# The low parts of the weight tiles, made once, stored to DRAM and loaded again by later token groups

## The chip, the cores and the metric

One Trainium2 chip, one of its cores. The time is the device time of one execution in microseconds; the smaller the better. All numbers are fp32, and the weights and activations that go through the projections are split into two parts so that TensorE's products keep fp32's precision.

## What is computed

One step of a diffusion backbone of one layer, for 128 prompt tokens and 2048 latent tokens of 1024 channels:

```python
def trunk_layer(x, cond, S0, ada_w, ada_b, norm_g, w_in, ...):
    mod = jax.nn.silu(cond) @ ada_w + ada_b
    shift, scale, gate = jnp.split(mod, 3, axis=-1)
    h = rmsnorm(x, norm_g) * (1 + scale[:, None]) + shift[:, None]
    p = h @ w_in                                   # one projection, columns for four branches
    qkv, g_a, beta_logit, a_logit, uv, g_b, x_c, g_c, x_d, g_d = jnp.split(p, _split_points(), axis=-1)
    y_a, S_new = deltanet_branch(...)              # gated delta rule: triangular solves, then a scan over chunks of 64
    y_b = sgu_branch(...)                          # spatial gating over 128 positions
    y_c = pool_branch(...)                         # centred averages of 2, 4, 8, 16
    y_d = fourier_branch(...)                      # real 2-D DFT over positions and channels
    out = jnp.concatenate([y_a, y_b, y_c, y_d], axis=-1) @ w_out
    return x + gate[:, None] * out, S_new
```

The change lies in `h @ w_in` alone: in how the weights of that product reach TensorE.

## The kernel before

**Tokens.** The 34 chunks of 64 tokens form three groups (0, 1, 2 with 12, 12 and 10 chunks). The split activations of one group, `hT`, lie in SBUF at a time; the weights are streamed past them. So every weight tile is brought in three times, once for each group.

**Weight tiles.** `load_w(src, n)` (L220 to L244) fills one slot of a ring of three slots in the SBUF tile BIG. A tile has 128 columns of all eight k blocks of 128 rows: 512 KB. It is loaded in two halves of four k blocks (`wst`, 256 KB each, a pool of two buffers, issued on SP's queue at L238). From each half two parts are made: `hi`, the value rounded to the fp32r type (a cast, on ACT at L242 in the first stages, on DVE at L240 once `Ring.late` is set), and `lo`, the rest `w - hi` (a subtract at L243: on DVE for the first half, on GpSimd, called POOL in the profile, for the second). `mm3` (L246 to L250) then makes three matmuls for each k block, hi by hi, hi by lo and lo by hi: 24 for one output chunk of 256 or more tokens. `proj_cm` (L486) works on two tiles at once and takes their chunks in turn, `proj_tm` (L475) on one. Two kinds of tiles are wider: `wxd` with 272 columns, and `wv` with 256 columns (1 MB, in two slots).

**Order of the work.** Phase A, up to about 450 us, goes through groups 0, 1 and 2 with wxd, the two pooling tiles `wxc_d` (which an earlier step has written to DRAM) and wt0 to wt5 (queries, keys, values), and makes the triangular solves of the delta rule (L725, L727). A later phase, called R here, goes through groups 2, 1 and 0 with the gate tiles wt6 to wt15 and `wv`. Between its projections stand the 32 steps of the scan over the latent chunks (L1015 to L1066, its matmuls at L1035, its loads of R and C at L1024 and L1026). The output projection (L1349 on, it uses L250 too) is last.

**What sets the order.** The kernel is written as a sequence of tiles, and a scheduler puts the instructions of each engine in order by a simulated time line and by priorities; `load_w` runs at a raised priority (`hp(OXv[1])`, 500), the matmuls at priority 0. Every load and store is issued on SP's one queue, in order: an issue that waits for a semaphore keeps back all that stand behind it. The completions use eight semaphores in turn, so each transfer also waits for the one eight before it.

Of the kernel before, what the change touches and what calls it, by code (L numbers as in the profile page):

```python
# [9 lines left out]
F32 = mybir.dt.float32  # L10
# [4 lines left out]
ALU = mybir.AluOpType  # L15
# [7 lines left out]
KC = D // 128  # L23
# [121 lines left out]
def tile_dit_step(ctx: ExitStack, tc: tile.TileContext, io: dict, dbg=None, stop=None):  # L145
    nc = tc.nc
# [5 lines left out]
    dram = ctx.enter_context(tc.tile_pool(name="dram", bufs=1, space=DR))  # L152
# [60 lines left out]
    def hp(o):  # L213
        return tc.high_priority(offset=o)
# [5 lines left out]
    def load_w(src, n):  # L220
        with hp(OXv[1]):
            ns = -(-n // SLOT)
            if ns == 1:
                s = Ring.order.pop(0)
                Ring.order.append(s)
            else:
                s = min(0, 1) if Ring.order.index(2) != 0 else 1
                for q in (s, s + 1):
                    Ring.order.remove(q)
                    Ring.order.append(q)  # L230
            hi = Wr[0][:, :, s * SLOT:s * SLOT + n]
            lo = Wr[1][:, :, s * SLOT:s * SLOT + n]
            for a in range(0, n, 136):
                w = min(136, n - a)
                for k0 in range(0, KC, 4):
                    ks = slice(k0, k0 + 4)
                    st = wst_p.tile([128, 4, SLOT], F32, tag="wst", name="wst")
                    nc.sync.dma_start(out=st[:, :, :w], in_=src[:, ks, a:a + w])  # L238
                    if Ring.late:
                        nc.vector.tensor_copy(hi[:, ks, a:a + w], st[:, :, :w])  # L240
                    else:
                        nc.scalar.activation(hi[:, ks, a:a + w], st[:, :, :w], AF.Copy)  # L242
                    (nc.vector if k0 == 0 else nc.gpsimd).tensor_tensor(lo[:, ks, a:a + w], st[:, :, :w], hi[:, ks, a:a + w].bitcast(F32), op=ALU.subtract)  # L243
            return hi, lo  # L244

    def mm3(out, lh, rh, ks=range(KC), first=0, last=KC - 1):  # L246
        with hp(OP):
# [122 lines left out]
    with tc.tile_pool(name="ada", bufs=3, reuse_waits="tile") as ada_p:  # L370
# [59 lines left out]
        p1 = x_prep([(i, 128) for i in range(3)], 0, 0, ada_p)  # L430
        a1 = ada_load(1)
        w_xd = load_w(io["wxd"], 272)
        with hp(300):
            mod_q(0, a0)
# [40 lines left out]
    def proj_tm(src, n, tiles, dst, w=None, done=()):  # L475
        hi, lo = w or load_w(src, n)
        for j, i in enumerate(tiles):
            if j < len(done):
                dst(j, i, done[j])
                continue  # L480
            ps = pj()
            mm3(ps[:, :n], [lambda k, q=q: hT[q][:, k, j * 128:(j + 1) * 128] for q in range(2)],
                [lambda k: hi[:, k], lambda k: lo[:, k]])
            dst(j, i, ps)

    def proj_cm(srcs, chunks, dsts):  # L486
        ws = [load_w(src, 128) for src in srcs]
        for (a, w) in chunks:
            for (hi, lo), dst in zip(ws, dsts):
                ps = pj()  # L490
                mm3(ps[:, :w], [lambda k: hi[:, k], lambda k: lo[:, k]],
                    [lambda k, q=q: hT[q][:, k, a:a + w] for q in range(2)])
                dst(a, w, ps)
                tick()
# [825 lines left out]
    op = [ctx.enter_context(tc.tile_pool(name="opa_", bufs=1, side="right", reuse_waits="tile"))]  # L1320
# [15 lines left out]
    for k in range(KC):  # L1336
        st = op[0].tile([128, D], F32, tag="wos", name="wos", bufs=2)
        nc.sync.dma_start(out=st, in_=io["wo"][k * 128:k * 128 + 128])
        st = st.rearrange("p (n j) -> p n j", j=256)
# [91 lines left out]
```

## Time and profile before

| | |
|---|---|
| three timed runs | 1191.8, 1192.86 (median), 1195.96 us |
| the profiled execution | 1198.78 us, of which the profiled span is 1197.0 us |
| mean granted TensorE clock | 0.919 of full speed |
| TensorE busy | 1046.3 us of the span (87%) |
| VectorE (DVE) busy | 818.9 us (68%) |
| GpSimd (POOL) busy | 433.2 us (36%) |
| bytes moved by SP's queue | 202.37 MB |

Busy times are sums over stages that differ: TensorE has almost no pause in some stretches of 50 us and stands for a quarter of others. The chain of waits, which is followed back from the last instruction, tells what the end of the span rested on; the windows tell, stage by stage, which engine is full.

### The profile page before, as it was taken

How to read it: one execution, taken by the hardware profiler on the slowest of the kernel's cores; microseconds unless marked ns; L12 is line 12 of the kernel's file. 1: busy time of each engine (PE TensorE's matmuls, PEld its weight loads, DVE VectorE, ACT ScalarE, POOL GpSimd, SP SyncE). 2: the span in 40 equal slices, each digit the busy share in tenths (PEclk: the TensorE clock that was granted, in tenths of full speed). 3: DMA queues.
4: the chain of work that ended last, by engine and by line, in shares of the span. 5: the costliest groups of instructions: out<-in, count | busy, mean ns of one | idle time of the engine just before them, and what ended most of it. 6: DMA issues, size and time to landing. Idle time of an engine off the chain costs nothing.

```text
span 1197.0 us, 27975 instructions
## 1 busy us (share of the span) xinstructions
PE 1046.3 (87%) x11351; PEld 954.6 (80%) x11351; DVE 818.9 (68%) x1837; ACT 386.2 (32%) x734; POOL 433.2 (36%) x436
## 2 busy tenths in 40 slices
PE   4689897888768789967988999888999889999997
PEld 1489786888757788955778888878899879999997
DVE  1547878699995799958865533672443398887765
ACT  1345566436675564131131111121111311111211
POOL 1338446633562245511132132232144444332212
PEclk7599897898978899988899999999999889999998
DMA  9799557854453655565268356578555655444331
GB/s 309 238 327 290 156 117 202 250 165 112 107 134 103 154 126 126 179 170 160 71 197 241 100 170 207 176 230 283 143 151 161 204 153 186 132 142 140 108 131 71
DMA packets 251395, 204.16 MB, mean 171 GB/s; under 512 B 109150, under 2 KB 218718, under 8 KB 251010
## 3 DMA queue, kind: packets, MB, share of 16 engines
q1 hardware_dynamic: 251266, 202.37, 57.7%
q8 instruction: 89, 1.46, 0.5%
q14 instruction: 40, 0.33, 0.1%
HBM read 138.86 MB, written 63.46 MB: 169 GB/s over the span
## 4 chain that ended last, share of the span: by engine, by line
PE 41%; DVE 27%; DMA 17%; issue 6%; ACT 4%; SPq 2%; POOL 2%; DVEq 0%; ACTq 0%; POOLq 0%
PE pj L250 32%; DMA wst<-in_wt_dram 4%; PE pa L1035 3%; DMA ada<-in_ada_dram 3%; DVE LL L727 3%; DVE acc L824 3%; DVE ltmp L725 3%; DMA pr<-in_cpr_dram 2%; DVE BIG L243 2%; DVE BIG L361 1%; DVE acc L871 1%; SPq L1024 1%; DVE BIG L240 1%; DVE BIG L362 1%; DVE LL L748 1%
## 5 line engine op out<-in xcount | busy, mean ns | idle before, releaser
L250 PE MATMUL pj<-BIG 128*128 128x256 f32 (+4 forms) x3888 | 630.8, 319 | 25.6 <-ACT raw L805 5.6
L250 PEld LDWEIGHTS pj<-BIG 128*128 128x128 f32 x3888 | 578.1, 201 | 50.7 <-issue 11.0
L250 PE MATMUL pj<-BIG,yh 128*128 128x256 f32 x1088 | 196.7, 286 | 1.6 <-ACT BIG L1340 0.8
L243 POOL TENSOR_TENSOR BIG<-wst,BIG 128x512 fp32r<-128x512 f32 (+1 forms) x66 | 93.3, 1414 | 215.2 <-DVE BIG L240 131.2
L250 PEld LDWEIGHTS pj<-BIG,yh 128*128 128x128 f32 x1088 | 164.7, 191 | 4.6 <-ACT BIG L1340 1.0
L250 PE MATMUL pj<-BIG,yl 128*128 128x256 f32 x544 | 140.8, 284 | 0.0
L250 PEld LDWEIGHTS pj<-BIG,yl 128*128 128x128 f32 x544 | 99.0, 191 | 0.4
L240 DVE CAST BIG<-wst 128x512 fp32r<-128x512 f32 (+2 forms) x72 | 35.0, 487 | 75.7 <-DMA wst<-in_wt_dram 35.4
L1398 POOL TENSOR_TENSOR z<-z,xs 128x1024 f32<-128x1024 f32 x16 | 40.3, 2521 | 75.8 <-DVE z L1390 66.0
L1042 POOL TENSOR_TENSOR gS<-S,sc_s 128x256 f32<-128x256 f32 x32 | 19.7, 616 | 132.1 <-DVE S L1057 109.1
L824 DVE SCALAR_TENSOR_TENSOR acc<-raw,prm,acc 128x768 f32<-128x768 f32 (+2 forms) x72 | 66.3, 942 | 1.6 <-ACT acc L822 1.6
L243 DVE TENSOR_TENSOR BIG<-wst,BIG 128x512 fp32r<-128x512 f32 (+1 forms) x66 | 49.8, 754 | 24.3 <-ACT BIG L242 20.7
L1359 ACT ACTIVATE yh<-yt 128x768 fp32r<-128x768 f32 (+1 forms) x34 | 20.5, 628 | 121.6 <-issue 65.5
L1204 ACT ACTIVATE g<-pj 128x256 f32<-128x256 f32 (+1 forms) x64 | 23.0, 397 | 109.6 <-PE pj L250 109.3
L725 DVE TENSOR_TENSOR ltmp<-LL 128x60 f32<-128x60 f32 (+14 forms) x90 | 55.5, 617 | 1.6
L727 DVE TENSOR_TENSOR LL<-LL,ltmp 128x60 f32<-128x60 f32 (+14 forms) x90 | 55.3, 615 | 1.5
L242 ACT ACTIVATE BIG<-wst 128x512 fp32r<-128x512 f32 (+1 forms) x60 | 37.7, 633 | 38.4 <-DMA wst<-in_wt_dram 17.9
L264 PE MATMUL pb<-ada,c 128*32 128x256 f32 x192 | 22.1, 566 | 31.7 <-DMA ada<-in_ada_dram 21.4
L1057 DVE TENSOR_TENSOR S<-pa,gS 128x256 f32<-128x256 f32 x34 | 14.3, 421 | 50.6 <-PE pc L1035 45.3
L1390 DVE TENSOR_TENSOR z<-pj,gbc 128x256 f32<-128x256 f32 x68 | 26.2, 420 | 29.1 <-PE pj L250 28.8
L362 POOL TENSOR_TENSOR BIG<-h,BIG 128x384 fp32r<-128x384 f32 (+2 forms) x28 | 29.1, 1041 | 44.5 <-DVE BIG L361 38.7
L1360 DVE TENSOR_TENSOR yl<-yt,yh 128x768 fp32r<-128x768 f32 (+1 forms) x34 | 40.4, 1206 | 4.1 <-ACT yh L1359 3.9
(280 smaller groups left out, 1690.2 us busy)
## 6 DMA issues: line engine op xcount, KB each, us to landing
wst<-in_wt_dram SPq DMA_DIRECT2D x96, 256.0 KB, 3.7
R<-rec_d SPq DMA_DIRECT2D x136, 128.0 KB, 3.0
ada<-in_ada_dram SPq DMA_DIRECT2D x24, 512.0 KB, 8.7
C<-com_d SPq DMA_DIRECT2D x68, 128.0 KB, 3.2
xs<-xs_d SPq DMA_DIRECT2D x16, 512.0 KB, 5.3
out_dram<-z SPq DMA_DIRECT2D x16, 512.0 KB, 3.0
x<-in_xs_dram SPq DMA_DIRECT2D x13, 512.0 KB, 6.4
xs_d<-x SPq DMA_DIRECT2D x13, 512.0 KB, 4.7
```

Of the source, the lines that this page charges most:

```text
L240: nc.vector.tensor_copy(hi[:, ks, a:a + w], st[:, :, :w])
L242: nc.scalar.activation(hi[:, ks, a:a + w], st[:, :, :w], AF.Copy)
L243: (nc.vector if k0 == 0 else nc.gpsimd).tensor_tensor(lo[:, ks, a:a + w], st[:, :, :w], hi[:, ks, a:a + w].bitcast(F32), op=ALU.subtract)
L250: nc.tensor.matmul(out, lh[a](k), rh[b](k), start=(k == first and i == 0), stop=(k == last and i == 2))
L362: (nc.gpsimd if f % 2 else nc.vector).tensor_tensor(hT[1][:, f, off:off + w], h, hi.bitcast(F32), op=ALU.subtract)
L725: nc.vector.tensor_tensor(tv, X[:, :, j, j + 1:32].unsqueeze(2).to_broadcast([128, 2, j, ni]), bc(X[:, :, 0:j, j], ni), op=ALU.mult)
L727: nc.vector.tensor_tensor(X[:, :, 0:j, j + 1:32], X[:, :, 0:j, j + 1:32], tv, op=ALU.add)
L824: nc.vector.scalar_tensor_tensor(o, raw[:, si + j:si + j + n], w[:, j:j + 1], o, op0=ALU.mult, op1=ALU.add)
L1035: nc.tensor.matmul(ps[o, q], lh(q)[hp], rh[hp, q])
L1360: nc.vector.tensor_tensor(yl[:, q], yt[:, q], yh[:, q].bitcast(F32), op=ALU.subtract)
L1390: nc.vector.tensor_tensor(z[:, ns], ps, gbc[:, cd, ns], op=ALU.mult)
L1398: nc.gpsimd.tensor_tensor(z, z, xs, op=ALU.add)
```

## The change

The first group that makes a tile still subtracts; when its `lo` is complete, one DMA writes it to a DRAM tile of its own (`lo_d`, 512 KB, or 1 MB for `wv`). For later groups the tile counts as `kept`: its `lo` is not computed but loaded from there, straight into the slot in BIG. The DMA for it is written ahead of the loads of `wst`, and it has to wait for the last matmul that reads the slot's old content. The halves of w are still loaded in every group, and `hi` is still cast from them. The 272 column tile is left as it was.

```diff
--- before.py
+++ after.py
@@ -230,6 +230,10 @@
                     Ring.order.append(q)
             hi = Wr[0][:, :, s * SLOT:s * SLOT + n]
             lo = Wr[1][:, :, s * SLOT:s * SLOT + n]
+            key = str(src)
+            kept = key in lo_d
+            if kept:
+                nc.sync.dma_start(out=lo.bitcast(F32), in_=lo_d[key])
             for a in range(0, n, 136):
                 w = min(136, n - a)
                 for k0 in range(0, KC, 4):
@@ -240,8 +244,14 @@
                         nc.vector.tensor_copy(hi[:, ks, a:a + w], st[:, :, :w])
                     else:
                         nc.scalar.activation(hi[:, ks, a:a + w], st[:, :, :w], AF.Copy)
-                    (nc.vector if k0 == 0 else nc.gpsimd).tensor_tensor(lo[:, ks, a:a + w], st[:, :, :w], hi[:, ks, a:a + w].bitcast(F32), op=ALU.subtract)
-            return hi, lo
+                    if not kept:
+                        (nc.vector if k0 == 0 else nc.gpsimd).tensor_tensor(lo[:, ks, a:a + w], st[:, :, :w], hi[:, ks, a:a + w].bitcast(F32), op=ALU.subtract)
+        if n != 272 and not kept:
+            lo_d[key] = dram.tile([128, KC, n], F32, name=f"lo_d{len(lo_d)}")
+            nc.sync.dma_start(out=lo_d[key], in_=lo.bitcast(F32))
+        return hi, lo
+
+    lo_d = {}
 
     def mm3(out, lh, rh, ks=range(KC), first=0, last=KC - 1):
         with hp(OP):
```

By the code that is 19 stores (8 in phase A for group 0, 11 in phase R for group 2; 18 of 512 KB and one of 1 MB) and 38 loads (16 in phase A for groups 1 and 2, 22 in phase R for groups 1 and 0; 36 of 512 KB and two of 1 MB). Of the 66 subtracts on DVE and the 66 on POOL 40 and 40 are gone. Lines of the changed kernel stand 4 (L233 to L249) or 10 (from L250 on) below those before: the store is L251 there, the load L236, wst L242, the casts L244 and L246, the subtract L248, the projections' matmul L260.

Where it shows in the order of the instructions, at four places. First DVE, in phase A, in a triangular solve (L725 and L727 before, L735 and L737 now). Before:

```order
L725 TENSOR_TENSOR ltmp<-LL 128x116
L727 TENSOR_TENSOR LL<-LL,ltmp 128x2x2x29
L725 TENSOR_TENSOR ltmp<-LL 128x168
L243 TENSOR_TENSOR BIG<-wst,BIG 128x4x128
L553 COPY P_1758<-pb 128x6x2x2
L727 TENSOR_TENSOR LL<-LL,ltmp 128x2x3x28
L725 TENSOR_TENSOR ltmp<-LL 128x216
```

Now:

```order
L735 TENSOR_TENSOR ltmp<-LL 128x116
L737 TENSOR_TENSOR LL<-LL,ltmp 128x2x2x29
L563 COPY P_1774<-pb 128x6x2x2
L735 TENSOR_TENSOR ltmp<-LL 128x168
L737 TENSOR_TENSOR LL<-LL,ltmp 128x2x3x28
L735 TENSOR_TENSOR ltmp<-LL 128x216
L737 TENSOR_TENSOR LL<-LL,ltmp 128x2x4x27
```

The subtract between the steps of the solve is gone; the other rows stand nearly as before.

Second SP, in phase A for group 0, where the second pooling tile and the next tokens (`xb`, `x`) are loaded. Before:

```order
L238 DMA wst<-wxc_d 128x4x128 x2
L355 DMA h_d<-h 128x384
L293 DMA xb<-in_xs_dram 128x1024 x3
L355 DMA h_d<-h 128x384 x3
L296 DMA pr<-in_cpr_dram 64x512
L238 DMA wst<-in_wt_dram 128x4x128
```

Now:

```order
L251 DMA lo_d_820<-BIG 1024x1x128
L242 DMA wst<-wxc_d 128x4x128 x2
L365 DMA h_d<-h 128x384
L303 DMA xb<-in_xs_dram 128x1024 x3
L365 DMA h_d<-h 128x384 x3
L303 DMA x<-in_xs_dram 128x1024
```

The store of the first tile's `lo` stands in the queue ahead of the load of the next tile and of the tokens.

Third SP with what each DMA waits for, in phase R for group 1 (DMAHW is one of the eight completion semaphores, the others are those of the engines). Before:

```order
L238 DMA wst<-in_wt_dram 128x4x128 [waits DMAHW5_49,DVE_49]
L238 DMA wst<-in_wt_dram 128x4x128 [waits DMAHW6_49,Pool_49]
L1026 DMA C<-com_d 128x256 [waits DMAHW7_49,PE_49]
L1026 DMA C<-com_d 128x256 [waits DMAHW0_49]
L238 DMA wst<-in_wt_dram 128x4x128 [waits DMAHW5_49,DMAHW1_49,Pool_49]
L1024 DMA R<-rec_d_78 64x512 [waits DMAHW2_49,PE_49]
```

Now:

```order
L242 DMA wst<-in_wt_dram 128x4x128 [waits DMAHW3_49,DMAHW0_49,DVE_49]
L1036 DMA C<-com_d 128x256 [waits DMAHW1_49,PE_49]
L1036 DMA C<-com_d 128x256 [waits DMAHW2_49]
L236 DMA BIG<-lo_d_6462 128x8x128 [waits PE_49]
L236 DMA BIG<-lo_d_5591 128x8x128 [waits DMAHW4_49,PE_49]
L242 DMA wst<-in_wt_dram 128x4x128 [waits DMAHW5_49,DVE_49]
L242 DMA wst<-in_wt_dram 128x4x128 [waits DMAHW6_49,DMAHW0_49,DVE_49]
```

Two loads of `lo` stand in a row, each waiting for TensorE to be done with its slot, and the next tile's `wst` and the scan's loads are behind them; the loads of `wst` wait for the cast on DVE and no longer for POOL's subtract.

Fourth TensorE, in phase R for group 0, ahead of the first use of tile wt13's `lo` (`pj` is a projection, `pa` and `pc` are the scan's). Before, the slot's old content is read last by the 20th matmul of the first row, and the new one first after 24 more matmuls:

```order
L250 MATMUL pj<-BIG 128x256 x23
L1035 MATMUL pa<-S,C 64x64 x2
L1035 MATMUL pc<-S,C 64x64 x2
L1035 MATMUL pa<-S,C 64x64
L1035 MATMUL pc<-S,C 64x64
```

Now the slot is read last by the 23rd matmul of the first row, and the new content first after the rest of the piece and 16 matmuls of the scan's, 49 matmuls in all:

```order
L260 MATMUL pj<-BIG 128x256 x24
L1045 MATMUL pa<-r,R 64x64 x8
L260 MATMUL pj<-BIG 128x256 x23
L1045 MATMUL pa<-xn,R 64x64
L1045 MATMUL pc<-xn,R 64x64
```

Between the last use of the slot and the first of the new `lo` there are now 24 matmuls of a projection and 24 of the scan.

## Rows read from the trace of the kernel before

**Rows 1.** The page, part 1 and the first line of part 4.

```profile
span 1197.0 us, 27975 instructions
...
PE 1046.3 (87%) x11351; PEld 954.6 (80%) x11351; DVE 818.9 (68%) x1837; ACT 386.2 (32%) x734; POOL 433.2 (36%) x436
...
PE 41%; DVE 27%; DMA 17%; issue 6%; ACT 4%; SPq 2%; POOL 2%; DVEq 0%; ACTq 0%; POOLq 0%
```

**Rows 2.** Windows: busy PE, PEld, DVE, ACT, POOL, clock, DMA share, GB/s.

```profile
50.00:100.00 50.00, 44.58 (x285) 42.52 (x286) 28.14 (x64) 23.47 (x46) 24.99 (x25) 0.90 0.87 290
100.00:150.00 50.00, 43.59 (x321) 41.98 (x320) 43.12 (x69) 29.25 (x53) 30.15 (x32) 0.93 0.69 199
...
250.00:300.00 50.00, 45.81 (x335) 43.11 (x334) 49.29 (x93) 25.53 (x43) 17.87 (x16) 0.93 0.47 117
300.00:350.00 50.00, 35.52 (x258) 31.22 (x256) 49.63 (x82) 33.24 (x52) 27.09 (x29) 0.84 0.55 130
...
400.00:450.00 50.00, 42.93 (x466) 41.01 (x466) 47.45 (x97) 30.67 (x60) 21.90 (x27) 0.87 0.64 147
...
850.00:900.00 50.00, 50.00 (x735) 46.89 (x735) 21.63 (x45) 6.92 (x17) 18.18 (x16) 1.00 0.50 148
```

**Rows 3.** Instructions of line L243 by engine: ns of one as min/median/max, start, shapes.

```profile
L243 DVE TENSOR_TENSOR BIG<-wst,BIG x66: 628/691/1748, 21.6 to 919.2; 128x512 fp32r<-128x512 f32 x54, 128x544 fp32r<-128x544 f32 x9, 128x480 fp32r<-128x480 f32 x3
L243 POOL TENSOR_TENSOR BIG<-wst,BIG x66: 1197/1298/2065, 26.0 to 923.7; 128x512 fp32r<-128x512 f32 x54, 128x544 fp32r<-128x544 f32 x9, 128x480 fp32r<-128x480 f32 x3
```

**Rows 4.** Timeline: start us, duration us, engine, line; first DVE, then POOL.

```profile
239.86 1.25 DVE L725 TENSOR_TENSOR ltmp<-LL 128x116 f32<-128x116 f32 x1
...
242.40 0.33 DVE L725 TENSOR_TENSOR ltmp<-LL 128x168 f32<-128x168 f32 x1
...
238.44 1.31 POOL L243 TENSOR_TENSOR BIG<-wst,BIG 128x512 fp32r<-128x512 f32 x1
239.70 1.27 POOL L297 TENSOR_TENSOR x<-x,pr 128x512 f32<-128x512 f32 x1
```

**Rows 5.** Chain of waits: start us, us, step; four of 22 steps of L243.

```profile
192.49 0.63 DVE BIG L243
...
442.48 0.60 DVE BIG L243
...
643.96 0.69 DVE BIG L243
...
793.08 0.70 DVE BIG L243
```

**Rows 6.** The page, parts 3 and 6, and the landing times of line L238.

```profile
q1 hardware_dynamic: 251266, 202.37, 57.7%
...
wst<-in_wt_dram SPq DMA_DIRECT2D x96, 256.0 KB, 3.7
...
xs<-xs_d SPq DMA_DIRECT2D x16, 512.0 KB, 5.3
...
DMA to landing us min/median/max: 2.6/3.4/8.0
```

**Rows 7.** Chain of waits, pace of TensorE.

```profile
821.64 2.93 PE pj L250 x23
...
828.84 0.61 PE pa L1035 x16
```

**Rows 8.** Chain of waits, three transfers in it.

```profile
82.25 7.06 DMA xb<-in_xs_dram
...
89.33 6.37 DMA x<-in_xs_dram
...
830.96 7.64 DMA wst<-in_wt_dram
```

**Rows 9.** Waits of SP's queue: us in total, times, longest.

```profile
SPq L238 <- DVE BIG L243: 89.1, 26, 10.0
SPq L238 <- POOL BIG L243: 68.5, 40, 3.9
```

## The prediction

> **What bounds the kernel now.** I read the page's first part and the head of its chain first [rows 1]: TensorE is busy 87% of the span, but the chain that ended last lies on it for only 41%, on DVE for 27% and on transfers for 17%. So there are three bounds at different places, and a mean says little about an edit that takes work from DVE and gives it to the DMA engines. The windows [rows 2] tell them apart. From 50 to 150 us the DMA engines are 69 to 87% busy: transfers lead. In three windows between 250 and 450 us DVE is busy 47 to 50 of 50 us and TensorE 35 to 46: DVE leads, with 4 to 14 us of TensorE idle in each. Later TensorE has whole windows without a pause (850 to 900 us). Two rows then show what the subtract of the low part costs and how: one on DVE takes 0.69 us, one on POOL 1.30 us [rows 3], and POOL's slows DVE too. At 239.86 us a DVE step of the solve with 116 columns takes 1.25 us while POOL's subtract and the next POOL operation run; at 242.40, with POOL between operations, the same step with 168 columns takes 0.33 us [rows 4].
>
> **Relief, phase A.** Sixteen of the kept tiles are used again by groups 1 and 2 there: 16 DVE and 16 POOL subtracts go. The chain of waits holds 13 steps of L243 for those tiles, 9.4 us in all; the first and the last stand in [rows 5]. To them come DVE steps that a POOL subtract stretches: one for each, 1.25 − 0.33 = 0.92 us by [rows 4], 16 × 0.92 = 15 us at most, nothing at least. DVE is full in about half of the stretch, so I take 8. The sum is 17 us. Not all of it comes through: in the windows where DVE is full TensorE itself has 4 to 14 us of idle time left, and once DVE is quicker the matmuls, the transfers and ACT's casts are late next. I take 70%: **−12 us**. Bounds: 0, if TensorE or a transfer ends every step at the same time as DVE did, and −24, 9.4 + 15.
>
> **Relief, phase R.** 24 more subtracts on each engine go. The chain has 9 steps of L243 there, 7.6 us [rows 5]. TensorE has little room in this phase (50.0 of 50 us at 850) and DVE is less than half busy there [rows 2], so I take half: **−4 us**, between 0 and −8. SP gains here as well: the loads of wst were kept back 68.5 us by POOL's subtracts and 89.1 us by DVE's [rows 9], and now wait for the cast alone. I give this no term of its own, since the two buffers are still held until a cast that waits for the slot; were it worth anything it would lie inside the −8.
>
> **The stores.** 18 × 0.5 + 1 = 10 MB, 10.5 in the trace's decimal unit. SP's queue took 57.7% of the sixteen engines' 1197 us for 202.37 MB [rows 6]: 3.41 us for each MB, so the stores take 36 us of all engines. If they cost what transfers cost on average, their share of the chain, 17%, it is **+6 us**. Lower bound 0: nobody waits for a store before the next group, and in phase R for group 2 nothing on the chain stands right behind one. Upper bound +14: the eight stores of phase A (4.2 MB, 14 us) lie where transfers lead. The first of them is issued just ahead of the next tokens' loads (the second place in the order), and those loads are on the chain, 7.06 and 6.37 us [rows 8], so whatever bytes stand in front of them are paid.
>
> **The loads: bytes.** 38 loads move 21 MB, 72 us of all engines by the same 3.41. At the chain's 17% that is 12 us; but they stand where the engines are about half busy (DMA shares of 0.47 to 0.64 in [rows 2] from 250 us on), and the loads behind them have two halves of slack, so I take a quarter: **+3 us**, between 0 and +12.
>
> **The loads: when they land.** A load of lo can't go out before the slot's last matmul. Before, the first half of a tile was there about a cast and a subtract after that; now all of it comes with one transfer of 512 KB. The trace has no such load. The nearest rows: a wst of 256 KB lands after 3.4 us (2.6 to 8.0), and 512 KB of xs after 5.3 [rows 6]; half a MB more at 3.41 us per MB puts it at 3.4 + 0.9 = 4.3 us. What the order leaves for it: in the tightest places (the fourth in the order) 24 matmuls of a projection and 24 of the scan stand between. At 2.93 us for 23 and 0.61 for each eight or so of the scan [rows 7] that is 4.3 to 4.9 us. The first tile of each pair has more than 15 us, counted in the same way. So 4.3 is just hidden and 5.3 costs 1 us each; fourteen tiles are placed so tightly (ten second tiles of a pair and wv in phase R, three in phase A), 14 us at most. I take **+2 us**, the price of two late ones in TensorE's full stretches. SP waits for TensorE with each of these loads, and what stands behind it is the next tile's wst and the scan's R and C (the third place). The wst has two buffers that are held until the cast anyway, and R and C have two as well: nothing more for that.
>
> The casts and the 24 matmuls of a chunk stay as they are, and with them all that TensorE does; nothing else moves but by the scheduler's order, which brings the scan slightly forward: no term.
>
> **The sum.** −12 − 4 + 6 + 3 + 2 = **−5 us**. The profiled execution took 1198.78 us, so 1193.8 by its count; the median of the three runs is 5.9 us below that execution, which puts the median after at **1188 us**. A measurement of this kernel tells about 0.3%, 3.6 us, from no change, so faster means below 1189.3 and slower above 1196.4.
>
> **A rule that speaks against it.** One row shows what a crowded memory does: a wst of 256 KB that needs 3.4 us as a rule took 7.64 us at 830.96 us, and TensorE's next step waited for it [rows 6, 8]. The Trainium skill, "DMA: Bandwidth & Descriptors", section "Latency and other measured facts", says as a rule that a memory access takes 0.2 us on average and 2 us under high load, the main part of a transfer's fixed cost. By that figure each load of lo under load would come an estimated 1.8 us later, 14 × 1.8 = 25 us at worst, where the rows' own 5.3 us gives 14. The 7.64 us agrees with its direction; no row separates a memory's latency from the rest of a transfer. It is priced by the rows as the second rival on that side.
>
> **The rivals.**
> The relief is off the path. TensorE, ACT's casts and the transfers end the steps that DVE ended, and −16 shrinks to −8 while the costs are +8: no change, **1193 us**. For it: the chain of a tuned stretch has many near ties, and TensorE's own work does not shrink. Against it: DVE is at 49.3 and 49.6 of 50 us in two windows and every POOL subtract there holds it up.
> Transfers end up on the path: **slower**. The place is phase A from 60 to 150 us for the stores, where the DMA share is 0.69 to 0.87 and the chain waits for x and xb, and the loads of lo of groups 1 and 2 after it. The price is +14 for the stores and +12 for the loads against a relief of −12: +14, **1207 us**. It decides from where more than about a third of the transfers' time is paid: 11 us of room (16 − 5) over the 36 of the stores is 30%. For it: [rows 8] are precisely loads that such a store stands ahead of. Against it: DMA shares of 0.47 to 0.64 in the windows after 250 us.
> The loads of lo are late at full TensorE: **slower**. The place is phase R, the second tile of every pair and wv. At the 5.3 us of xs each of fourteen is 1 us late, +14; with stores +6, loads +3 and a relief of −10, since waits for lo take up what the subtracts gave: +13, **1206 us**. It decides from a landing of about 4.3 us. For it: the window at 850 has no idle time to hide it, and the 7.64 us of a wst. Against it: the median of 3.4.
>
> **How the numbers follow.** A gain as summed: 0.44. No change: 0.21. Transfers on the path: 0.25. Late loads: 0.10. So faster 0.44, same 0.21, slower 0.35. The forecast's own range is 1172 (relief in full, 9.4 + 8 + 7.6 = 25, with costs of 4) to about 1192. The range of 8 in 10 has to take in both slower cases to where their prices end, so it goes from 1172 to 1212, 5 us above the 1207.
>
> **What would show it.** In the profile after: L243's rows halved to 26 and 26; DVE's busy time down by some 30 us and POOL's by 50; the steps of the solve at 0.3 to 0.4 us where they took 1.25; SP's bytes up by about 31 MB, and the DMA share of the windows up to 150 us by a few hundredths. The gain has to stand between 180 and 450 us, with the projections of groups 1 and 2 reached 10 us earlier. If x and xb land later than 7 us, the stores are paid; if TensorE waits for a DMA into BIG from 590 us on, the loads are late. The forecast is wrong if the first 200 us grow by more than 6 us, if phase A isn't shorter, or if a load of 512 KB takes over 5 us at the median.

## The result, and the profile after

The changed kernel takes 1202.41 us (median of 20 runs) against 1195.09 us before (20 runs); the ratio is 1.0068 with a 95% interval of 1.0050 to 1.0087. The ratio is that of the means, without one run of the kernel before that took 1402.6 us. The changed kernel is slower by 8 us, inside the range of the forecast and on the other side of no change. In the other ratios of this text, too, a difference in us is the ratio less one times 1193 us, about what the kernel before took beside each experiment. An interval of 0.002 to 0.0035 to either side is 2 to 4 us, so the difference of two such ratios is uncertain by 3 to 5 us.

The page of the changed kernel: the span, part 1, the queue of part 3 and the first line of part 4.

```profile
span 1202.9 us, 27947 instructions
...
PE 1034.0 (86%) x11351; PEld 948.3 (79%) x11351; DVE 783.4 (65%) x1797; ACT 386.1 (32%) x734; POOL 379.2 (32%) x396
...
q1 hardware_dynamic: 310546, 233.83, 66.8%
...
PE 43%; DVE 26%; DMA 19%; ACT 4%; issue 4%; SPq 2%; POOL 1%; DVEq 0%; ACTq 0%; POOLq 0%
```

Beside [rows 1, 6]: DVE has lost 35 us of busy time and POOL 54, as removed; TensorE 12; SP's queue moves 233.83 MB in place of 202.37 and holds the DMA engines for 66.8% of the span. In the chain DVE has lost a point and transfers have won two.

Where the time went shows first in three lines that mark the way: the convolutions of phase A (first and last start of L824, now L834), the gates of phase R (L1204, now L1214) and the output projection (L1390, now L1400). One line each: engine, operation, ns as min/median/max, first and last start in us, shapes. Before:

```profile
L824 DVE SCALAR_TENSOR_TENSOR acc<-raw,prm,acc x72: 339/1003/2228, 127.4 to 464.2; 128x768 f32<-128x768 f32 x36, 128x512 f32<-128x512 f32 x18, 128x128 f32<-128x128 f32 x18
...
L1204 ACT ACTIVATE g<-pj x64: 364/384/447, 475.3 to 947.0; 128x256 f32<-128x256 f32 x48, 128x320 f32<-128x320 f32 x16
...
L1390 DVE TENSOR_TENSOR z<-pj,gbc x68: 409/423/427, 974.1 to 1188.8; 128x256 f32<-128x256 f32 x68
```

After:

```profile
L834 DVE SCALAR_TENSOR_TENSOR acc<-raw,prm,acc x72: 337/1005/2233, 123.0 to 444.0; 128x768 f32<-128x768 f32 x36, 128x512 f32<-128x512 f32 x18, 128x128 f32<-128x128 f32 x18
...
L1214 ACT ACTIVATE g<-pj x64: 365/384/448, 457.7 to 956.7; 128x256 f32<-128x256 f32 x48, 128x320 f32<-128x320 f32 x16
...
L1400 DVE TENSOR_TENSOR z<-pj,gbc x68: 410/423/427, 986.0 to 1194.6; 128x256 f32<-128x256 f32 x68
```

Phase A ended 20 us earlier (444.0 for 464.2), and the first gates of phase R came 18 us earlier. The last gate came 10 us later, and the output projection began 12 us later. So the gain was there, larger than the forecast had it, and phase R lost it and more: some 27 us between the first gate and the last. The output projection then won 6 us back: it takes 209 us from its first step to its last in place of 215, so that the end comes 6 us later. (These are single executions; that of the kernel before was 4 us above its median and that of the changed kernel 2.)

The windows of 50 us answer to [rows 2] (busy PE, PEld, DVE, ACT, POOL, clock, DMA share, GB/s); 600:650 is new here, and its row of the kernel before follows.

```profile
50.00:100.00 50.00, 43.95 (x287) 41.27 (x286) 29.37 (x64) 22.66 (x43) 22.96 (x23) 0.91 0.85 284
100.00:150.00 50.00, 45.76 (x347) 44.08 (x346) 44.16 (x71) 31.36 (x55) 30.40 (x34) 0.97 0.83 243
...
250.00:300.00 50.00, 45.10 (x351) 42.40 (x350) 47.34 (x82) 27.84 (x43) 17.77 (x19) 0.97 0.65 162
300.00:350.00 50.00, 34.02 (x260) 30.32 (x258) 48.98 (x99) 36.57 (x60) 25.79 (x32) 0.83 0.65 152
...
400.00:450.00 50.00, 46.26 (x407) 43.82 (x398) 49.27 (x108) 31.57 (x60) 19.44 (x31) 1.00 0.81 193
...
600.00:650.00 50.00, 37.67 (x430) 34.12 (x429) 33.39 (x85) 8.06 (x24) 14.96 (x9) 0.86 0.98 285
...
850.00:900.00 50.00, 47.06 (x639) 42.53 (x638) 15.68 (x34) 7.81 (x19) 13.27 (x13) 0.97 0.66 201
```

```profile
600.00:650.00 50.00, 44.53 (x685) 40.03 (x684) 29.68 (x59) 14.07 (x34) 13.27 (x11) 0.96 0.84 237
```

From 600 to 650 us the DMA engines are 98% busy (84% before), and TensorE does 37.7 us of work in place of 44.5. At 850 us, where TensorE had no pause at all, it now has 3 us of them. In the three windows between 250 and 450 us DVE is about as full as it was, 47 to 49 of 50 us: it gets further in that time, but it still leads there.

The subtracts, and what SP's loads of wst waited for (beside [rows 3, 9]):

```profile
L248 DVE TENSOR_TENSOR BIG<-wst,BIG x26: 647/692/1960, 21.5 to 576.3; 128x512 fp32r<-128x512 f32 x18, 128x544 fp32r<-128x544 f32 x7, 128x480 fp32r<-128x480 f32 x1
L248 POOL TENSOR_TENSOR BIG<-wst,BIG x26: 1213/1416/2023, 25.9 to 577.7; 128x512 fp32r<-128x512 f32 x18, 128x544 fp32r<-128x544 f32 x7, 128x480 fp32r<-128x480 f32 x1
...
SPq L242 <- DVE BIG L244: 28.9, 18, 5.1
...
SPq L242 <- POOL BIG L248: 19.1, 10, 3.7
```

In these rows more than half of the waits are gone: 48 us of SP's time in place of 158. Others have taken their place in part, such as 11.3 us for ACT's casts, so that all waits of these loads together fell from 242 to about 175 us. And the solve's steps still take 1.3 us where POOL is at work, beside [rows 4]; that work is now the positional add on the tokens alone (L307, L308), which before stood there beside the subtract (L297 in [rows 4]). A step of 216 columns that starts as POOL's adds end takes 0.38 us. DVE's lines, then POOL's:

```profile
229.16 1.28 DVE L735 TENSOR_TENSOR ltmp<-LL 128x116 f32<-128x116 f32 x1
...
235.83 0.38 DVE L737 TENSOR_TENSOR LL<-LL,ltmp 128x216 f32<-128x216 f32 x1
...
229.00 1.30 POOL L308 TENSOR_TENSOR x<-x,cpc 128x512 f32<-128x512 f32 x1
...
234.16 1.40 POOL L308 TENSOR_TENSOR x<-x,cpc 128x512 f32<-128x512 f32 x1
```

Three places in the chain of waits of the changed kernel show what phase R is held up by: start us, us, step. First the hand-over from group 2 to group 1:

```profile
598.60 8.40 DMA wst<-in_wt_dram
...
607.02 5.27 DMA C<-com_d
...
619.75 6.12 DMA hr<-h_d
...
627.33 6.08 DMA hr<-h_d
```

A wst that takes 8.40 us, the scan's C and then two loads of group 1's activations (hr), 6.12 and 6.08 us: from 598.6 to 633.4 us the chain hardly touches TensorE. Then two loads of lo, and what TensorE (its weight loads, PEld, and its matmuls) waited for lo in the whole span:

```profile
850.19 11.30 DMA BIG<-lo_d
...
908.36 5.70 DMA BIG<-lo_d
...
PEld pj L260 <- DMA BIG<-lo_d: 10.2, 8, 2.1
...
PE pj L260 <- DMA BIG<-lo_d: 8.4, 6, 1.9
```

A load of lo that takes 11.30 us stands in the chain until 861 us, in a stretch that was solid TensorE work before. That is how long the transfer took, and not how long TensorE stood still: no wait for lo is longer than 2.1 us. The weight loads' waits and the matmuls' stand beside each other, so that the two sums are not to be added.

### The profile page after: what moved, and what is told of

Same layout as the page of the kernel before. It is cut to its first block, busy times and chain, and to the rows that moved or that the text cites. A ratio compares the mean times of both kernels' runs of the same rounds, so it can differ in the third digit from the quotient of the medians.

```text
span 1202.9 us, 27947 instructions
## 1 busy us (share of the span) xinstructions
PE 1034.0 (86%) x11351; PEld 948.3 (79%) x11351; DVE 783.4 (65%) x1797; ACT 386.1 (32%) x734; POOL 379.2 (32%) x396
## 3 DMA queue, kind: packets, MB, share of 16 engines
q1 hardware_dynamic: 310546, 233.83, 66.8%
## 4 chain that ended last, share of the span: by engine, by line
PE 43%; DVE 26%; DMA 19%; ACT 4%; issue 4%; SPq 2%; POOL 1%; DVEq 0%; ACTq 0%; POOLq 0%
PE pj L260 34%; DMA wst<-in_wt_dram 4%; DVE LL L737 4%; DVE ltmp L735 3%; PE pa L1045 3%; DVE acc L834 3%; DMA BIG<-lo_d 3%; DMA pr<-in_cpr_dram 2%; DMA ada<-in_ada_dram 2%; DMA Pf<-pf_d 1%; DMA hr<-h_d 1%; DVE BIG L371 1%; DMA h_d<-h 1%; DVE BIG L248 1%; DVE LL L728 1%
## 5 line engine op out<-in xcount | busy, mean ns | idle before, releaser
L260 PE MATMUL pj<-BIG 128*128 128x256 f32 (+4 forms) x3888 | 623.0, 317 | 31.5 <-DMA BIG<-lo_d 8.4
L260 PEld LDWEIGHTS pj<-BIG 128*128 128x128 f32 x3888 | 572.8, 199 | 54.2 <-DMA BIG<-lo_d 10.2
L260 PE MATMUL pj<-BIG,yh 128*128 128x256 f32 x1088 | 197.8, 287 | 7.3 <-DVE z L1400 4.8
L260 PEld LDWEIGHTS pj<-BIG,yh 128*128 128x128 f32 x1088 | 166.6, 192 | 10.1 <-DVE z L1400 4.9
L260 PE MATMUL pj<-BIG,yl 128*128 128x256 f32 x544 | 142.2, 284 | 0.0
L260 PEld LDWEIGHTS pj<-BIG,yl 128*128 128x128 f32 x544 | 100.3, 192 | 0.3
L244 DVE CAST BIG<-wst 128x512 fp32r<-128x512 f32 (+2 forms) x72 | 36.8, 515 | 78.1 <-DMA wst<-in_wt_dram 36.6
L834 DVE SCALAR_TENSOR_TENSOR acc<-raw,prm,acc 128x768 f32<-128x768 f32 (+2 forms) x72 | 67.9, 960 | 6.4 <-ACT acc L832 6.3
L248 POOL TENSOR_TENSOR BIG<-wst,BIG 128x512 fp32r<-128x512 f32 (+2 forms) x26 | 38.7, 1487 | 100.1 <-DVE BIG L244 78.5
L1214 ACT ACTIVATE g<-pj 128x256 f32<-128x256 f32 (+1 forms) x64 | 23.0, 397 | 112.0 <-PE pj L260 111.5
L737 DVE TENSOR_TENSOR LL<-LL,ltmp 128x60 f32<-128x60 f32 (+14 forms) x90 | 54.4, 604 | 1.6
L735 DVE TENSOR_TENSOR ltmp<-LL 128x60 f32<-128x60 f32 (+14 forms) x90 | 53.8, 598 | 1.5
L1370 DVE TENSOR_TENSOR yl<-yt,yh 128x768 fp32r<-128x768 f32 (+1 forms) x34 | 47.6, 1429 | 9.9 <-ACT yh L1369 9.8
L246 ACT ACTIVATE BIG<-wst 128x512 fp32r<-128x512 f32 (+1 forms) x60 | 38.0, 635 | 43.1 <-DMA wst<-in_wt_dram 22.5
L1400 DVE TENSOR_TENSOR z<-pj,gbc 128x256 f32<-128x256 f32 x68 | 26.3, 420 | 30.2 <-PE pj L260 29.8
L1063 ACT ACTIVATE xn<-pa 128x256 f32<-128x256 f32 x34 | 13.1, 384 | 97.0 <-PE pa L1045 96.9
```

The costliest lines, as they stand in the source:

```text
L260: nc.tensor.matmul(out, lh[a](k), rh[b](k), start=(k == first and i == 0), stop=(k == last and i == 2))
L735: nc.vector.tensor_tensor(tv, X[:, :, j, j + 1:32].unsqueeze(2).to_broadcast([128, 2, j, ni]), bc(X[:, :, 0:j, j], ni), op=ALU.mult)
L737: nc.vector.tensor_tensor(X[:, :, 0:j, j + 1:32], X[:, :, 0:j, j + 1:32], tv, op=ALU.add)
L834: nc.vector.scalar_tensor_tensor(o, raw[:, si + j:si + j + n], w[:, j:j + 1], o, op0=ALU.mult, op1=ALU.add)
L1370: nc.vector.tensor_tensor(yl[:, q], yt[:, q], yh[:, q].bitcast(F32), op=ALU.subtract)
L1400: nc.vector.tensor_tensor(z[:, ns], ps, gbc[:, cd, ns], op=ALU.mult)
```

## The experiments

Kernels that leave out or replace part of the product are named as such in their expectations. The first four take parts of the change; the scheduler makes a new order for each, and so it does for the last two.

**Phase A alone, phase R alone.**

```diff
-        if n != 272 and not kept:
+        if n != 272 and not kept and not Ring.late:
```

> Only phase A keeps its low parts (8 stores, 16 loads of 512 KB); phase R subtracts as before. In the trace of the changed kernel phase A ended some 14 to 19 us earlier than before and everything had been lost by the end of R. Theory 1 (the loads of lo in R eat the gain: the DMA engines are full at 600 us and TensorE waits for lo between 730 and 910): the gain of A stays, about -12 us against before, ratio 0.990 (0.984 to 0.995). Theory 2 (the lead of A is lost in R whatever the loads do, since R starts on other bounds such as the ada loads and the solve of group 2): no change, ratio 1.000 (0.996 to 1.003).

The other has `and Ring.late` there.

> Only phase R keeps its low parts (11 stores, 22 loads); phase A subtracts as before. Theory 1: R alone loses what the trace showed between 470 and 985 us, about 20 us, ratio 1.017 (1.010 to 1.024). Theory 2: R's loads cost only what TensorE waits for them directly, 8 us by the page of the changed kernel, ratio 1.007 (1.002 to 1.010).

Phase A alone: 1182.24 us, ratio 0.9888 (0.9859 to 0.9918), 13 us faster than before. Phase R alone: 1199.76 us, ratio 1.0029 (1.0005 to 1.0054), 3.5 us slower. For A the number of theory 1 came out, though this run does not tell R's loads from R's order. For R neither number was met in full, though 1.0029 lies within theory 2's bounds. And the two don't add: −13 and +3.5 make −10, while both together cost +8. The three marks of the kernel with phase A alone:

```profile
L834 DVE SCALAR_TENSOR_TENSOR acc<-raw,prm,acc x72: 336/1004/2229, 124.2 to 445.7; 128x768 f32<-128x768 f32 x36, 128x512 f32<-128x512 f32 x18, 128x128 f32<-128x128 f32 x18
...
L1214 ACT ACTIVATE g<-pj x64: 366/385/446, 458.9 to 929.8; 128x256 f32<-128x256 f32 x48, 128x320 f32<-128x320 f32 x16
...
L1400 DVE TENSOR_TENSOR z<-pj,gbc x68: 407/422/427, 957.5 to 1175.0; 128x256 f32<-128x256 f32 x68
```

Phase A ends as in the changed kernel (445.7); its lead is still 17 us at the last gate and at the output projection.

**Stores alone.**

```diff
-            kept = key in lo_d
+            kept = False
...
-        if n != 272 and not kept:
+        if n != 272 and key not in lo_d:
```

> All 19 stores are made, nothing is loaded, every group subtracts as before: the price of the stores alone. My sum had +6 us (0 to +14). Theory 1 (the loads are the cost, stores hide): +2 us, ratio 1.002 (0.999 to 1.005). Rival (the stores lead, as the chain of waits at 82 and 89 us could suggest): +8 us or more, ratio above 1.006.

1198.42 us, ratio 1.0033 (1.0008 to 1.0058): +4 us, within theory 1's bounds.

**Neither subtracts nor transfers for the later groups.**

```diff
-                nc.sync.dma_start(out=lo.bitcast(F32), in_=lo_d[key])
+                pass
...
-            nc.sync.dma_start(out=lo_d[key], in_=lo.bitcast(F32))
+            pass
```

> Later groups neither subtract nor load the low part, and nothing is stored: the matmuls read what lies in the slot, so this part of the product is left out. It prices the relief of DVE, POOL and their waits alone. My sum had 16 us (0 to 32): ratio 0.987 (0.975 to 0.997). Theory 1 needs the relief to be at least what phase A showed, 14 us and more, with something from R as well: 0.978 to 0.988. Theory 2 (the lead is lost in R anyway) gives 0.995 to 1.000.

1187.38 us, ratio 0.9943 (0.9918 to 0.9967): only 7 us, which lies between the numbers of the two theories and is less than phase A alone gains with its 24 transfers. The first mark says that already phase A gained little here:

```profile
L834 DVE SCALAR_TENSOR_TENSOR acc<-raw,prm,acc x72: 336/1004/2225, 126.0 to 456.4; 128x768 f32<-128x768 f32 x36, 128x512 f32<-128x512 f32 x18, 128x128 f32<-128x128 f32 x18
```

It ends at 456.4, not at 444 to 446, although DVE, POOL and SP have less to do. So a kernel with less work can be the slower one, and the order had to be held fixed before anything could be priced.

**The same order, other sizes.** The next kernels take the program after the scheduler has ordered it, and change nothing but the sizes of the named instructions. Each engine's order and the semaphores stay. For the loads:

```diff
+    out, n = [], 0
+    for line in nc.print().split(b"\n"):
+        if b'"opcode": "DMACopy"' in line and b'"lineno": 236' in line:
+            n += 1
+            if n in range(1, 39):
+                line = re.sub(rb"\[(\d+), 1024\], \[1, 1\], \[1, (\d+)\]", lambda m: b"[%d, 128], [1, 1], [1, %d]" % (8 * int(m[1]), int(m[2])), line)
+                line = line.replace(b"[408, 8]", b"[408, 1]")
+        out.append(line)
+    nc = type(nc).parse(b"\n".join(out))
```

`range(17, 39)` are the loads of phase R, `range(1, 17)` those of phase A.

> The changed kernel in exactly its order, with every wait; only the size of its 38 loads of lo is changed after the order is made: each brings the first of the eight k blocks, 64 KB in place of 512, so the rest of that part of the product is made from what lies in the slot. Theory P (the loads' bytes and late landing turned phase A's gain into a loss): about -14 us against the kernel before, ratio 0.987 (0.981 to 0.993). Theory O (the order that the scheduler made for R is slow by itself: the loads of the next group's activations stand behind the scan's loads): 1.000 to 1.006, as little changes.

> As the one with all loads made small, but only the 22 loads of phase R; phase A's 16 are whole. Theory P with R as the place: nearly the same gain, ratio 0.989 (0.984 to 0.994). If phase A's loads cost something as well: 3 us or more above the kernel with all loads small. Theory O: 1.001 to 1.007.

> The changed kernel in exactly its order, only the 16 loads of phase A small, the 22 of phase R whole. All small against only R's small differed by 9 us, R's small against none by 13. If the two parts add: 0.999 (0.996 to 1.002). If phase A's lead is lost in R whatever its size, as the loads of R then wait for the same things: 1.005 (1.002 to 1.008).

All loads small: 1179.92 us, ratio 0.9883 (0.9855 to 0.9912). Only R's small: 1188.90 us, 0.9959 (0.9935 to 0.9983). Only A's small: 1192.63 us, 0.9998 (0.9975 to 1.0022). With none small it is 1.0068. So the loads of phase A cost 8 us (1.0068 to 0.9998) to 9 (0.9959 to 0.9883), those of phase R 13 (1.0068 to 0.9959) to 14 (0.9998 to 0.9883), and the two add: the loads turn a gain of 14 us into a loss of 8. Theory P holds for the loads; R's small alone missed its first number (0.989), as phase A's loads cost something too. What the order does is not told by these three. Where R's loads cost is told in part by the same window in two of these kernels, first all loads small, then only A's small:

```profile
600.00:650.00 50.00, 43.69 (x561) 40.52 (x563) 30.53 (x88) 8.95 (x27) 7.85 (x5) 0.88 0.74 207
```

```profile
600.00:650.00 50.00, 38.42 (x450) 35.45 (x450) 31.89 (x87) 7.61 (x23) 10.26 (x6) 0.86 0.92 262
```

TensorE does 5 us less there, at a DMA share of 0.92 in place of 0.74. By these two executions the hand-over has less than half of the 13 us, and the rest comes later.

**The subtracts at the order of the kernel before.** In the same way, with the kept tiles' subtracts cut to one column of 128; the other kernel cuts POOL's alone.

```diff
+    for j, k in zip(subs, KEPT):
+        if k:
+            txt[j] = re.sub(rb"\[1, (128|120|136)\]", b"[1, 1]", txt[j]).replace(b"[1, 544]", b"[1, 4]")
```

> The kernel before in exactly its order, with every wait; only the 80 subtracts of the kept tiles (40 on DVE, 40 on POOL) are made small after the order is made, one column of 128 each, so that part of the product is left out. It prices the relief alone at a fixed order. My sum had 16 us (0 to 32): ratio 0.987 (0.978 to 0.995). Rival (the gain of phase A came from another order, not from the subtracts): 0.995 to 1.000.

> The kernel before in exactly its order; of the kept tiles' subtracts only POOL's 40 are made small, DVE's 40 are whole. With all 80 small the ratio was 0.980. My sum priced POOL's part in phase A as up to 15 us of held up DVE steps, 8 taken. If POOL's share is the larger: 0.987 (0.983 to 0.991). If DVE's own subtracts make the relief: 0.995 (0.992 to 1.000).

All 80: 1169.18 us, ratio 0.9802 (0.9770 to 0.9835), a relief of 24 us. POOL's 40 alone: 1177.50 us, 0.9883 (0.9853 to 0.9913), 14 of the 24. With POOL's alone small the busy times are:

```profile
PE 1042.8 (89%) x11351; PEld 951.1 (81%) x11351; DVE 795.1 (68%) x1837; ACT 387.0 (33%) x734; POOL 389.7 (33%) x436
```

DVE's busy time is 24 us less than before (818.9), though none of its instructions was changed: that is the stretch that POOL's subtracts put on DVE's steps. SP's waits for POOL's subtracts fell as well, from 68.5 to 50.3 us; no run tells how much of the 14 us came each way. The marks, and the subtracts, of the kernel with all 80 small:

```profile
L824 DVE SCALAR_TENSOR_TENSOR acc<-raw,prm,acc x72: 338/1005/2228, 126.7 to 445.6; 128x768 f32<-128x768 f32 x36, 128x512 f32<-128x512 f32 x18, 128x128 f32<-128x128 f32 x18
...
L1204 ACT ACTIVATE g<-pj x64: 364/384/443, 456.4 to 919.5; 128x256 f32<-128x256 f32 x48, 128x320 f32<-128x320 f32 x16
...
L1390 DVE TENSOR_TENSOR z<-pj,gbc x68: 412/424/426, 944.9 to 1159.6; 128x256 f32<-128x256 f32 x68
...
L243 DVE TENSOR_TENSOR BIG<-wst,BIG x66: 154/170/1675, 21.0 to 891.6; 128x4 fp32r<-128x4 f32 x40, 128x512 fp32r<-128x512 f32 x18, 128x544 fp32r<-128x544 f32 x7, 128x480 fp32r<-128x480 f32 x1
L243 POOL TENSOR_TENSOR BIG<-wst,BIG x66: 208/369/3358, 25.0 to 896.1; 128x4 fp32r<-128x4 f32 x40, 128x512 fp32r<-128x512 f32 x18, 128x544 fp32r<-128x544 f32 x7, 128x480 fp32r<-128x480 f32 x1
```

The lead is 19 us at the end of phase A and grows to 29 us at the output projection: phase R gains some 10 us as well. (These are single executions; that of the kernel before was 4 us above its median, so 29 us here stand for 24 by the runs. A small subtract still takes 0.17 us on DVE and 0.37 on POOL, so 24 us is a little short of the whole.)

**What is left: stores, order, waits.** Stores and loads small together; and the loads small with TensorE not waiting for them, where 33 of its 38 waits are lowered to the transfer before on the same semaphore and the load copies lo_d onto itself, so that the slot is free of it:

```diff
+                if k in loads:
+                    return m[0].replace(b'"wait_value": ' + m[2], b'"wait_value": %d' % (int(m[2]) - 16))
```

> The changed kernel in exactly its order, with loads and stores of lo both made small after the order is made (one k block of eight), so that part of the product is made from what lies there. With the loads alone made small the ratio was 0.9883. If the stores cost at this order what they cost alone (+4 us): 0.985 (0.981 to 0.988). If they are hidden: 0.988. What then still separates it from the kernel before with its subtracts made small (0.980) is the order itself and the waits of the small loads, 6 to 9 us.

> The changed kernel in exactly its order, with all loads of lo small (64 KB, lo_d copied onto itself in DRAM) and 33 of TensorE's 38 waits for them lowered, so that neither their bytes nor their landing counts (that part of the product is made from what lies in the slot); they still stand in SP's queue and wait there for their slot. What is left against the kernel before with small subtracts (0.980) is the order that the scheduler made, and the queue. Theory O2 (the order costs 8 to 12 us): 0.989 (0.986 to 0.992), as with small loads that TensorE waits for. Theory W2 (waits even for the small loads cost it): 0.982 (0.978 to 0.986).

Stores small as well: 1182.07 us, 0.9920 (0.9889 to 0.9950), above both expected numbers and no faster than with the loads alone small; at this order the stores cost nothing that shows. Without the waits: 1183.38 us, 0.9906 (0.9871 to 0.9941), no faster either. That is theory O2. The three kernels without the loads' bytes lie at −14, −10 and −11 us, where the subtracts alone gave −24: **10 to 14 us are lost to the order that the scheduler made**, with the loads' places in SP's queue in it. SP still waits 12.4 us for slots ahead of the small loads; what of the 10 to 14 is that, and what the order on the engines, no run here tells. That a new order alone can cost as much, the kernel without subtracts and loads shows, which has no such loads in its queue. The marks of the last one:

```profile
L834 DVE SCALAR_TENSOR_TENSOR acc<-raw,prm,acc x72: 334/1004/2226, 123.0 to 435.3; 128x768 f32<-128x768 f32 x36, 128x512 f32<-128x512 f32 x18, 128x128 f32<-128x128 f32 x18
...
L1214 ACT ACTIVATE g<-pj x64: 366/384/448, 450.4 to 930.9; 128x256 f32<-128x256 f32 x48, 128x320 f32<-128x320 f32 x16
...
L1400 DVE TENSOR_TENSOR z<-pj,gbc x68: 410/423/427, 959.9 to 1169.0; 128x256 f32<-128x256 f32 x68
```

It leaves phase A 29 us ahead of the kernel before, and begins the output projection only 14 us ahead, where the small subtracts in the old order went from 19 to 29. So the new order of phase A was the better one by some 10 us (less what the small subtracts there still take), and the new order of phase R the worse one by some 25; the output projection, 209 us in place of 215, gives 6 back. Two lines show where phase R begins to lose. The first load of group 1's activations goes out at the same time in both, first the small subtracts in the old order, then the last kernel, so that the 10 us that the new order had won in phase A are gone by then:

```profile
L1196 SPq DMA_DIRECT2D hr<-h_d x16: 359/428/1453, 584.4 to 763.7; - x16
```

```profile
L1206 SPq DMA_DIRECT2D hr<-h_d x16: 365/380/1799, 584.0 to 766.7; - x16
```

And ahead of it, between 445 and 610 us, TensorE waits 14 us for DVE in group 2's solve, where with the small subtracts it waits 7.4 (5.6 for L748 and 1.8 for a subtract). The changed kernel has the same two waits, 8.5 and 6.5 us, and of the kernels with another order only that with hr first has the second one:

```profile
PE pa L775 <- DVE LL L758: 7.9, 1, 7.9
PE pa L775 <- DVE rt L327: 6.1, 1, 6.1
```

It belongs to the order of phase R, but no run takes it away, so its price in the whole is not shown.

**Bytes or waits, in phase R.** R's 22 loads whole, but copied from lo_d onto itself, with 17 of TensorE's waits for them lowered.

> The changed kernel in exactly its order; the 22 loads of phase R move all their bytes at the same places of the queue and wait for the same slots, but copy lo_d onto itself in DRAM, and 17 of TensorE's waits for them are lowered to the transfer before on the same semaphore, so that TensorE doesn't wait for them (that part of the product is made from what lies in the slot). Theory W (the cost of R's loads, 13 us, is TensorE waiting for lo that lands late): ratio 0.997 (0.994 to 1.000). Theory B (it is their bytes, which delay hr, wst, R and C): 1.004 (1.001 to 1.008).

1196.39 us, ratio 1.0039 (1.0015 to 1.0063). Of the 13 us that R's loads cost, 3 to 4 are TensorE's waits for lo (1.0068 to 1.0039, hardly clear of noise), 9 to 10 remain with the bytes alone (1.0039 to 0.9959). Theory B. TensorE's waits for lo that are left are phase A's (the copies no longer write BIG):

```profile
PEld pj L260 <- DMA BIG<-lo_d: 2.6, 2, 1.7
...
PE pj L260 <- DMA BIG<-lo_d: 2.1, 2, 1.4
```

One doubt remains: these copies write to DRAM and not to SBUF. They hold the DMA engines for as long, 67.1% of the span for 66.8%.

**The next group's activations first.**

```diff
     def r_load(gi):
-        with hp(OXv[0]):
+        with hp(3000):
```

> The changed kernel whole, but the loads of the next group's activations (hr) get a priority that puts them ahead of the scan's loads in SP's queue. Theory O: most of the 16 us that the changed kernel lost between 550 and 620 us come back, ratio 0.993 (0.988 to 0.998). Theory P: the bytes are the same, so it stays where the changed kernel is, 1.003 to 1.009.

1202.68 us, ratio 1.0069 (1.0044 to 1.0094), where the changed kernel is. The loads of hr stood behind the scan's in the hand-over, but to bring them forward alone gains nothing in the end. The test is a weak one, as this kernel has an order of its own: in its profiled execution the output projection began at 981.4 us in place of 986.0, so that 5 us did come back, but it took 213 us in place of 209, and the last step came at 1194.2 us for 1194.6. So that place was not shown to be the cause by itself.

**Half of it, in phase A.**

```diff
-                nc.sync.dma_start(out=lo.bitcast(F32), in_=lo_d[key])
+                nc.sync.dma_start(out=lo[:, 4:].bitcast(F32), in_=lo_d[key])
...
-                    if not kept:
+                    if k0 == 0 or not kept:
```

> Phase A alone keeps its low parts, and only the half that POOL subtracts (8 stores and 16 loads of 256 KB); DVE subtracts its half in every group. If POOL's subtracts are what slows DVE, the relief is nearly that of both halves at half the transfers: ratio 0.986 (0.981 to 0.991). If DVE's own 0.69 us are what counted: 0.994 (0.990 to 0.999).

1194.92 us, ratio 1.0017 (0.9993 to 1.0042): no gain, and outside both expectations, with half the transfers and, by the runs at fixed order, some half of the relief. It has an order of its own from phase A on, and what the half is worth can't be told from that order.

Of all these phase A alone is the fastest that computes the whole: it beats the kernel before by 1.1% and the changed one by 1.8%.

## Why the prediction was wrong, step by step

The forecast was −16 of relief, +6, +3 and +2 of costs, −5 in all. At a fixed order the runs give −24 of relief, about 0 for the stores, +18 to +22 for the loads and, for the order, what is left: +10 to +14. The three kernels without the loads' bytes (−14, −10 and −11) divide the 32 us between −24 and +8 into these two parts, so the sum closes by its making, and a larger share of the one is a smaller share of the other. Two steps failed: the loads' bytes, put at +3, and the order, put at nothing.

| term | forecast | bounds given | measured | from |
|---|---|---|---|---|
| relief | −16 | 0 to −32 | −24 | subtracts small, order of before |
| stores | +6 | 0 to +14 | about 0 (alone, with a new order, +4) | stores small, stores alone |
| loads, bytes | +3 | 0 to +12 | +17 to +19, with A's landing | A's loads small, R's loads unwaited |
| loads, landing | +2 | 0 to +14 | +3 to +4 in R | R's loads unwaited |
| order, with SP's queue | none | none | +10 to +14 | what is left with the loads small, with and without waits |

**Relief: the mechanism right, the size too small.** The two parts, DVE's own subtracts and the DVE steps that POOL's stretch, are both real: POOL's subtracts are worth 14 of the 24 us, 0.35 us for each of 40, and DVE's the other 10, a difference that the intervals don't make sure. I had counted POOL's part in phase A only and cut the whole by 30 and 50%. Phase A ran 19 us ahead with small subtracts, against the 17 that I had cut to 12; phase R, where I saw too little idle time to gain more than 4 us, gained some 10. TensorE's full windows there were not the whole phase.

**Stores: too dear.** The chain at 82 and 89 us [rows 8] was the ground for up to 14 us. After the change that chain still has such transfers, 85.68 and 93.51 us:

```profile
85.68 7.82 DMA h_d<-h
...
93.51 7.47 DMA x<-in_xs_dram
```

The first convolution still started 4 us earlier than before (123.0 for 127.4, the marks above), and with the stores small the kernel was no faster. The forecast's sign for paid stores, x later than 7 us, appeared without the cost. From 100 to 150 us the DMA share rose from 0.69 to 0.83, and the stretch took the bytes.

**The loads' bytes: the first step that failed.** I priced 72 us of transfers at the chain's 17%, 12 us, and then took a quarter of that, since the mean DMA share after 250 us was 0.47 to 0.64. The upper bound of 12 didn't hold either: 8 to 9 in phase A and 9 to 10 in phase R. By the forecast's own 3.41 us for each MB, A's loads are 29 us of all engines and R's 43, so that in both phases they cost about 30% of that time (8 to 9 and 13 to 14, late landing included), where I had taken 4%, or 7% with the landing. A mean share of the DMA engines says nothing about a hand-over. From 600 to 650 us the next group's activations, the halves of the next tiles, the scan's records and now 1.5 MB of lo are wanted; the engines were 84% busy there already, a row that I gave no weight. But the hand-over is only a part: the cost is about the same share in A, and in R most of it comes later.

**The loads' landing: the right rival, a small price.** Loads were late as the third rival had it: two of them stand in the chain at 850 and 908 us with 11.30 and 5.70 us, and 10 us of the weight loads' idle time ends with one. By the run without waits it cost 3 to 4 us in phase R, within my bounds. That my +2 came near it is in part luck, as the working has two slips. What was added to the 256 KB of a wst is another 256 KB, and not half a MB; the 0.9 us are right. And [rows 7] has 0.61 us for 16 matmuls of the scan and not for eight, so the room was 3.7 to 4.0 us and not 4.3 to 4.9. By my own 4.3 us each of the fourteen loads would have been 0.3 to 0.6 us late, 5 to 9 us in all.

**The order: the term I set to nothing, the second step that failed.** I read the places where the order had changed and called the scan's earlier steps "no term". The kernel that neither subtracts nor loads later took 0.9943 with the scheduler's new order, and the kernel before with the same subtracts made small 0.9802 with its old one: 17 us between two orders of almost the same work. By the sum, this and not the loads alone made the sign: with an order as good as before, −24 and +18 to +22 would have been a gain of 2 to 6 us. That is an estimate from the terms, partly within the noise, and no run shows it. What in the order of phase R costs it is open. TensorE's longer wait in group 2's solve is one candidate. The hand-over to group 1 is another, but putting hr first there won nothing in the end.

**The rivals.** The second, transfers on the path, came nearest: 1207 us, for the wrong place (the stores in phase A) and partly the right one (the loads). Its number is in part luck: its +14 for the stores was not paid, and what the loads cost beyond its +12, and the order, stood in for them. None of the rivals had a new order in it.

## What to carry to other kernels

Ask of each added transfer who waits behind it: here 36 us of stores cost nothing that shows, and 72 us of loads about 30% of their time in both phases, whatever the mean DMA share said. Where a scheduler orders the work, an edit is two changes, its own and a new order; to price the edit, keep the order and change sizes after it is made. And a change that pays in one phase and not in another can be made in that phase alone, as here.

## What the runs showed of the hardware that was not expected

Forty small subtracts on POOL cost 14 us, beside 10 for their twins on DVE (a difference within the noise), although POOL was busy for 36% of the span; with them small, DVE was busy 24 us less. Taking such POOL work away does not free DVE's steps where other POOL work stands beside them, as at 229.16 us. And a mean of 50 us hides what one transfer meets: the load that took 11.30 us stands in a window with a DMA share of 0.66, but in ten us with 0.91:

```profile
850.00:860.00 10.00, 9.64 (x126) 7.83 (x124) 2.75 (x7) 1.71 (x4) 1.31 (x2) 1.00 0.91 295
```

The wst of 7.64 us in [rows 8] stands in such a stretch too, in the kernel before:

```profile
830.00:840.00 10.00, 5.14 (x85) 4.68 (x87) 3.04 (x10) 1.13 (x4) 1.90 (x2) 0.97 1.04 312
```
